# A hybrid S5 / gated DeltaNet / MoE layer: Toeplitz loads and input loads on another DMA queue, w_mod tiles in other buffers, S5's readout weights moved, one clearing on VectorE

## The chip, the cores and the metric

One core of one Trainium2 chip. The metric is device time in microseconds. The kernel before takes 1488.81 us (median of three runs).

## The reference, cut to what matters

One layer over 256 latent tokens and 256 context tokens, width 1024, float32. The computation, shortened:

```python
mod = silu(c) @ w_mod + b_mod          # shift, scale, gate of both norms; the same for c_ctx
h  = rmsnorm(x, norm1) * (1 + sc1) + sh1          # latent tokens
hc = rmsnorm(ctx, norm1) * (1 + csc1) + csh1      # context tokens
u, qkv, gate, b_raw, a_raw, br = split(h @ w_in)
q, k, v = split(silu(short_conv(qkv)))
ya = glu(s5(u))                        # bidirectional complex diagonal SSM, starts from the context's state
yb = gated_norm(gdn(q, k, v), gate)    # bidirectional chunked DeltaNet, a triangular solve per chunk of 64
x = x + gt1 * ((sig(br_a) * (ya @ w_branch_a) + sig(br_b) * (yb @ w_branch_b)) @ w_out)
x = x + gt2 * moe(rmsnorm(x, norm2) * (1 + sc2) + sh2)   # 32 experts, top 4
return rmsnorm(x, norm_f)
```

## The kernel before, in words

Weights stream from HBM in tiles of 128 x 2048 (1 MB), issued by SP. They land in the five `ld` buffers or in one of the 1 MB registers that `r()` names (`R0`, `PB`, `XC`, ...). A register or buffer comes free when its last reader is done, and a load for it waits until then.

**Start.** `mod1` multiplies silu(c) by eight tiles of `w_mod` (`wm`, line 226), adds `b_mod` into `modrow` and transposes it. `load_x` and `load_h` load and normalise the tokens and transpose them (`xn`, 32 transposes). `modulate` then forms the input `h` and its high part `hh`. From there on PE multiplies `h` and `hh` by tiles of `w_in` (`win`, line 609). ScalarE rounds each piece to its high part and VectorE takes the rest (`wsp`). Each projection `u`, `k`, `v`, `q`, `gate`, `br` is a run of blocks of 512 columns of weights. A block on all tokens is 24 products, and after `lat_only` (latent tokens alone) 16. Sixteen steps of the second `w_mod` half lie between blocks (`mod` in ORDER).

**S5.** `s5_prep` makes powers of the diagonal. `s5_P` writes the drive weights of direction 0 into registers PA and PB, of direction 1 into R2 and V (`pt` are the pieces that PE transposes). `s5_in` multiplies them with U, which goes through DRAM (`us`). `s5_R0` and `s5_R1` form the readout weights R from CC and PD, with 24 operations of 128x512 each on POOL (ENG_R). `s5_scan` runs on VectorE, `s5_steps` (31 steps on `XL`, which the scan fills) on POOL. `s5_K` multiplies BB with R (256 products) into `KS`, which ScalarE stores to DRAM in two halves (`kd`, line 543). `s5_T` loads the Toeplitz tiles T back from there with sixteen DMAs of 128 KB, eight from SP's and eight from ScalarE's queue (line 577). `s5_out` multiplies T with U, and R with XL.

**DeltaNet.** `l2k` normalises k (`sq` on ScalarE, `rnk` on POOL, transposes on PE), `l2q` does it for q (`rnq`). `gdn_a` makes the chunk matrix A, stores it (`ad`) and loads it as M. It clears Y on POOL (lines 1092 and 1093), and 31 steps on VectorE solve for Y. `yd` stores Y, `gdn_b1` reads it back as Yb. Eight scan steps follow, then the branches and `merge`.

**Experts.** `merge` starts the stream of 403 MB of expert weights. Tile after tile goes into a ring of 19 buffers (`WREG`), each as soon as its buffer is free.

**What sets the order.** SP's DMAs are issued in program order. On the other engines a scheduler fixes one static order from priorities. ORDER is the sequence of the program and `name@p*n` calls a part n times with its priority lowered by p. An engine works through its order without overtaking.

Of the kernel before, what the change touches and what calls it, by code (L numbers as in the profile page):

```python
# [27 lines left out]
class Kern:  # L28
# [166 lines left out]
    ENG_P, ENG_R, ENG_E = "GVGGVVVV", "GGGGGGGG", "VVGV"  # L195
    ORDER = """proj_ba u*5 mod*2 gdn_e k mod k mod k mod k mod s5_C s5_in0 s5_in1 s5_R0 s5_scan l2k gdn_a
        v mod v mod v mod v mod lat_only s5_steps s5_R1 q mod q mod q mod q mod l2q s5_K s5_T mod*2 gate*4
        br@3000*8 s5_out gdn_b0 br@3000*8 gdn_b1 s5_glu@500 ba@500*8"""

    def mod1(self):  # L200
# [9 lines left out]
        def run(cb, nb, tag):  # L210
# [3 lines left out]
            def step(j, b):  # L214
# [10 lines left out]
                t = self.ld("wm")  # L225
# [72 lines left out]
    def load_h(self):  # L298
# [3 lines left out]
        junk = self.r("H0", "junk")[:, :D]  # L302
# [56 lines left out]
    def s5_load(self):  # L359
        nc, I, wk = self.nc, self.I, self.wk  # L360

        self.L = self.r("R2", "L")[:, :768].rearrange("p (a b) -> p a b", b=32)
        nc.sync.dma_start(self.L[:, 0], dram(I["s5_lam_re"], 0, [[32, 128], [1, 32]]))
        nc.sync.dma_start(self.L[:, 1], dram(I["s5_lam_im"], 0, [[32, 128], [1, 32]]))
        for a in range(2):
            nc.sync.dma_start(self.L[64 * a:64 * a + 64, 2], dram(I["s5_log_step"], 32 * a, [[0, 64], [1, 32]]))
# [2 lines left out]
        for i, nm in enumerate(("s5_b_re", "s5_b_im")):
            nc.sync.dma_start(self.raw[:, i], dram(I[nm], 0, [[512, 128], [1, 512]]))  # L370

    def s5_loadc(self):
        for i, nm in enumerate(("s5_c_re", "s5_c_im")):
            self.nc.sync.dma_start(self.raw[:, 2 + i], dram(self.I[nm], 0, [[512, 128], [1, 512]]))
# [102 lines left out]
    def s5_R1(self):  # L477
        self.s5_R(1, ("R0", "R1"))
# [26 lines left out]
    def s5_K(self):  # L505
# [3 lines left out]
        KS = self.r("PB", "KS")  # L509
# [79 lines left out]
    S5L = 1  # L589
    WIN0 = 0  # L590
# [474 lines left out]
    def gdn_a(self):  # L1065
# [727 lines left out]
```

## Time and profile before

| | |
|---|---|
| runs of the kernel before, us | 1487.31, 1488.81, 1489.29 |
| profiled execution, its own time | 1497.49 us |
| its span | 1495.7 us |
| mean granted clock of PE | 0.948 |
| busy: PE, DVE, ACT, POOL | 1347.7, 572.4, 267.5, 210.7 us |
| DMA bytes | 474.06 MB |

The profiled execution took 8.68 us more than the median of the runs. Differences are read inside the profiled execution and then taken off the median. The timeline gives for a group of like instructions its start, its length and in brackets the idle time ahead of it with what ended it. The windows give busy time by engine in a stretch. The groups give busy time, mean length and idle time of all instructions of one kind.

### The profile page before, as it was taken

To read this page: it belongs to the slowest core of one execution; us is meant where nothing else is said; L and a number is where in the kernel's file an instruction comes from. 1 tells how busy PE (TensorE), PEld (TensorE's weight loads), DVE (VectorE), ACT (ScalarE), POOL (GpSimd) and SP (SyncE) were. 2 spreads that over 40 slices of the span, in tenths; PEclk is the share of its full clock that TensorE was granted. 3 is DMA by queue.
4 is the path that set the end of the run, shared out by engine and by line. 5 is a ranking of instruction groups with operands and counts; after the bars stand their busy time and mean duration, and the time that the engine had idled before them with its cause. 6 is when DMAs were issued, how large, how long until landed. Compare 5 with 4: busy or idle time off the path is not lost. (4 is left out here: it accounts for less than half of the span.)

```text
span 1495.7 us, 18843 instructions
## 1 busy us (share of the span) xinstructions
PE 1347.7 (90%) x7583; PEld 631.3 (42%) x7583; DVE 572.4 (38%) x1097; ACT 267.5 (18%) x592; POOL 210.7 (14%) x324
## 2 busy tenths in 40 slices
PE   4799796399989989999999999999999999999975
PEld 1365664277958543333333333333333333333221
DVE  4869988365334432223223123123222212221223
ACT  3443331124410011101111111111111101110001
POOL 1725687512000000000000000000000000000000
PEclk9799897699989989999999999999999999999996
DMA  9283162932184889999999999999999999999992
GB/s 336 75 215 131 68 197 59 191 100 78 61 204 179 305 317 381 422 421 420 419 421 421 420 420 420 421 420 420 420 421 421 420 420 421 421 421 420 420 420 109
DMA packets 92689, 474.06 MB, mean 317 GB/s; under 512 B 23984, under 2 KB 28317, under 8 KB 40757
## 3 DMA queue, kind: packets, MB, share of 16 engines
q1 hardware_dynamic: 72925, 461.11, 77.9%
q10 hardware_dynamic: 19672, 11.68, 3.7%
q8 instruction: 62, 1.02, 0.3%
q14 instruction: 30, 0.25, 0.0%
HBM read 468.61 MB, written 4.15 MB: 316 GB/s over the span
## 5 line engine op out<-in xcount | busy, mean ns | idle before, releaser
L79 PE MATMUL ps<-w,xT 128*64 128x512 f32 x2048 | 488.2, 602 | 6.5 <-DMA w<-in_w_gate_up_dram 6.4
L79 PEld LDWEIGHTS ps<-w,xT 128*64 128x64 f32 x2048 | 138.2, 137 | 269.8 <-issue 244.2
L79 PE MATMUL ps<-w,aT 128*64 128x512 f32 x1024 | 233.9, 600 | 10.5 <-DMA w<-in_w_down_dram 9.7
L1729 DVE SCALAR_TENSOR_TENSOR od<-ps,cs,gt 128x512 f32<-128x512 f32 x32 | 24.0, 751 | 478.0 <-PE ps L79 478.0
L79 PEld LDWEIGHTS ps<-w,aT 128*64 128x64 f32 x1024 | 72.1, 138 | 165.0 <-issue 128.2
L79 PE MATMUL ps<-h,wsp 128*128 128x512 f32 (+1 forms) x480 | 112.9, 375 | 2.9 <-DVE gx L94 2.0
L94 DVE TENSOR_TENSOR x<-x,ps 128x512 f32<-128x512 f32 x128 | 84.0, 684 | 65.8 <-PE ps L79 65.8
L1525 POOL CAST selsd<-biad 128x128 fp32r<-128x128 f32 x32 | 9.4, 294 | 700.0 <-PE ps L79 700.0
L97 ACT ACTIVATE odh<-od 128x512 fp32r<-128x512 f32 x31 | 19.5, 630 | 424.4 <-DVE od L1729 424.4
L79 PEld LDWEIGHTS ps<-h,wsp 128*128 128x128 f32 x480 | 82.0, 199 | 29.9 <-issue 12.4
L94 DVE TENSOR_TENSOR wsp<-win,wsp 128x512 fp32r<-128x512 f32 x72 | 58.5, 841 | 42.2 <-ACT wsp L97 41.9
L79 PE MATMUL ps<-h,oh 128*64 128x512 f32 x248 | 63.0, 604 | 0.0
L97 ACT ACTIVATE wsp<-win 128x512 fp32r<-128x512 f32 x72 | 41.3, 622 | 84.0 <-PE ps L79 42.4
L79 PE MATMUL ps<-hh,wsp 128*128 128x512 f32 x192 | 53.6, 411 | 1.3 <-DVE wsp L94 1.3
L97 ACT ACTIVATE sgm<-gt 128x512 f32<-128x512 f32 x32 | 20.1, 629 | 174.1 <-DVE gt L1702 174.1
L79 PE MATMUL ps<-wm,sc 128*32 128x512 f32 x192 | 34.4, 733 | 12.8 <-DMA wm<-in_w_mod_dram 12.8
L706 DVE SCALAR_TENSOR_TENSOR cacc<-raw,cols,cacc 128x512 f32<-128x512 f32 (+1 forms) x48 | 43.6, 908 | 3.2 <-ACT cacc L97 3.0
L1702 DVE TENSOR_SCALAR gt<-ps 128x512 f32<-128x512 f32 x32 | 22.1, 692 | 58.8 <-PE ps L79 58.8
L97 ACT ACTIVATE aT<-ps 128x512 f32<-128x512 f32 x32 | 19.1, 597 | 140.0 <-PE ps L83 140.0
L79 PEld LDWEIGHTS ps<-hh,wsp 128*128 128x128 f32 x192 | 35.1, 192 | 18.9 <-issue 10.0
L1525 POOL CAST selsg<-biad 128x256 fp32r<-128x256 f32 x32 | 13.9, 433 | 191.0 <-PE ps L79 184.8
L79 PE MATMUL ps<-odh,ST 64*128 64x512 f32 x124 | 31.7, 505 | 6.0 <-ACT odh L97 6.0
(370 smaller groups left out, 1497.2 us busy)
## 6 DMA issues: line engine op xcount, KB each, us to landing
w<-in_w_gate_up_dram SPq DMA_DIRECT2D x242, 1024.0 KB
w<-in_w_down_dram SPq DMA_DIRECT2D x121, 1024.0 KB
wm<-in_w_mod_dram SPq DMA_DIRECT2D x24, 1024.0 KB
win<-in_w_in_dram SPq DMA_DIRECT2D x18, 1024.0 KB
w<-in_w_gate_up_dram SPq DMA_DIRECT2D x28, 512.0 KB
w<-in_w_down_dram SPq DMA_DIRECT2D x14, 512.0 KB
wo<-in_w_out_dram SPq DMA_DIRECT2D x4, 1024.0 KB
wa<-in_w_branch_a_dram SPq DMA_DIRECT2D x4, 512.0 KB
```

The lines of the kernel that those rows point to most:

```text
L79: self.nc.tensor.matmul(out, lhsT, rhs, start=start, stop=stop, **kw)
L94: (eng or self.nc.vector).tensor_tensor(out, a, b, op=op)
L97: self.nc.scalar.activation(out, in_, func, **kw)
L706: nc.vector.scalar_tensor_tensor(acc[:, rows], rt[:, rows, k:k + 64], sc, acc[:, rows], op0=OP.mult, op1=OP.add)
L1525: nc.gpsimd.tensor_copy(v.rearrange("p (n s) -> p n s", s=CAP), dup[:, x:x + n, None].to_broadcast([128, n, CAP]))
L1702: V.tensor_scalar(gt, pz[0], 7.0, None, op0=OP.min)
L1729: V.scalar_tensor_tensor(od, self.pd, self.cs, k.gt2, op0=OP.mult, op1=OP.mult)
```

## The change

- `mod1`'s first five `w_mod` tiles go to the registers R0, R1, H0, H1 and GA, the last three to `ld`. Tokens, S5's small inputs and the second set of small vectors are loaded from ScalarE's queue. S5's c weights are loaded with its b weights. The loads of `wba` and of two `w_in` tiles stand right behind `w_mod`. `mod1`'s ending is a function of its own, called after `load_h`.
- `s5_P(1)` comes ahead of `s5_P(0)`, and `s5_C` and `s5_R0` come right behind both. Some of their operations change between POOL and VectorE (ENG_P), and one product on the DeltaNet side goes from POOL to VectorE (ENG_E).
- ORDER: `s5_R1` and `s5_steps` come ahead of v. `s5_K` and `s5_T` come ahead of q, where they stood behind `l2q`. `s5_out` and `gdn_b0` come ahead of the gates, whose priority is lowered like `br`'s.
- R1 goes to PB and R2, KS to R0, T to R0 and R1. The second XB goes to register K.
- All sixteen loads of T come from ScalarE's queue. Y is cleared on VectorE.

```diff
-        self.load_h()
+        self.s5_load()
+        self.smalls1()
         self.mod1()
         self.wins, self.winq, self.pair = self.win_order(), [], {}
+        self.ba_load()
         for _ in range(self.WIN0):
             self.win_load()
-        self.s5_loadc()
+        self.load_h()
+        self.mod1_end()
         self.modulate()
         self.s5_prep()
-        self.P = [self.s5_P(0), self.s5_P(1)]
+        self.P = [None, self.s5_P(1)]
+        self.P[0] = self.s5_P(0)
+        self.s5_C()
+        self.s5_R0()
...
-    ENG_P, ENG_R, ENG_E = "GVGGVVVV", "GGGGGGGG", "VVGV"
-    ORDER = """proj_ba u*5 mod*2 gdn_e k mod k mod k mod k mod s5_C s5_in0 s5_in1 s5_R0 s5_scan l2k gdn_a
-        v mod v mod v mod v mod lat_only s5_steps s5_R1 q mod q mod q mod q mod l2q s5_K s5_T mod*2 gate*4
-        br@3000*8 s5_out gdn_b0 br@3000*8 gdn_b1 s5_glu@500 ba@500*8"""
+    ENG_P, ENG_R, ENG_E = "GVGVVGVV", "GGGGGGGG", "VVVV"
+    ORDER = """proj_ba u*5 mod*2 gdn_e k mod k mod k mod k mod s5_in0 s5_in1 s5_scan l2k gdn_a s5_R1 s5_steps
+        v mod v mod v mod v mod lat_only s5_K s5_T q mod q mod q mod q mod l2q mod*2 s5_out gdn_b0
+        gate@1000*4 br@3000*16 gdn_b1 s5_glu@500 ba@500*8"""
...
-                t = self.ld("wm")
+                t = self.r(regs[j], "wm") if j < len(regs) else self.ld("wm")
...
-        for j, f in enumerate(run(0, 1, "p5")):
+        for f in run(0, 1, "p5", ("R0", "R1", "H0", "H1", "GA")):
             f()
-            if j == self.S5L:
-                self.s5_load()
-                self.smalls1()
...
-        self.rows(nc.sync, lambda t, a, b: self.xt[a:b, t], I["x"], True)
+        self.rows(nc.scalar, lambda t, a, b: self.xt[a:b, t], I["x"], True)
...
-        self.s5_R(1, ("R0", "R1"))
+        self.s5_R(1, ("PB", "R2"))
...
-        KS = self.r("PB", "KS")
+        KS = self.r("R0", "KS")
...
-        self.T = [self.r(x, "T").rearrange("p (g k) -> p g k", g=16) for x in ("PB", "R2")]
-        for hf, eng in ((0, nc.sync), (1, nc.scalar)):
+        self.T = [self.r(x, "T").rearrange("p (g k) -> p g k", g=16) for x in ("R0", "R1")]
+        for hf, eng in ((0, nc.scalar), (1, nc.scalar)):
...
-    WIN0 = 0
+    WIN0 = 2
...
-        nc.gpsimd.memset(Y, 0.0)
-        nc.gpsimd.memset(Y.rearrange("p i j -> p (i j)")[:, ::33], 1.0)
+        V.memset(Y, 0.0)
+        V.memset(Y.rearrange("p i j -> p (i j)")[:, ::33], 1.0)
...
-            X = self.r(("GA", "R3")[grp], "XB").rearrange("p (x i) -> p x i", i=128)
+            X = self.r(("GA", "K")[grp], "XB").rearrange("p (x i) -> p x i", i=128)
```

How it moves instructions, in three places. The first is PE's order at the start, before: the last `w_mod` group stands between two groups of transposes of S5's pieces (`pt`).

```order
L79 MATMUL ps<-wm,sc 32x512 x16
L83 MATMUL ps<-ident,pt_411 128x128 x4
L79 MATMUL ps<-wm,sc 32x512 x4
L83 MATMUL ps<-ident,pt_412 128x128 x4
L83 MATMUL ps<-ident,modrow 128x128 x4
L79 MATMUL ps<-hh_122,wba 32x512
```

The same place in the changed kernel:

```order
L79 MATMUL ps<-wm,sc 32x512 x8
L83 MATMUL ps<-ident,rows 128x128
L83 MATMUL ps<-ident,xn 128x128 x4
L83 MATMUL ps<-ident,pt_417 128x128 x4
L83 MATMUL ps<-ident,xn 128x128 x4
L83 MATMUL ps<-ident,modrow 128x128 x4
L83 MATMUL ps<-ident,xn 128x128 x8
L83 MATMUL ps<-ident,pt_418 128x128 x4
```

The last `w_mod` groups now stand ahead of S5's pieces, and one group of pieces, of the direction that is now made first, stands ahead of `modrow`.

The second place is PE's order ahead of T's products with U, before. BB with R is `s5_K`, `sq`, `rnq` belong to `l2q`, and vT are transposes for `gdn_b0`.

```order
L79 MATMUL ps<-ident,rnq 128x128 x8
L83 MATMUL ps<-ident,vT 128x128 x3
L79 MATMUL ps<-ident,vT 64x128 x4
L83 MATMUL ps<-ident,vT 128x128 x2
L79 MATMUL ps<-ident,vT 64x128 x2
L79 MATMUL ps<-T,U 32x128 x18
```

In the changed kernel `s5_K` (with `rnk` and the key products put among its rows) comes right behind v. Its first transposes of `rnk` stand behind 8 of its 256 products. From the second `q` block's end on the order is (h with `wsp` is q):

```order
L79 MATMUL ps<-wm,sc 32x512 x4
L79 MATMUL ps<-h_266,wsp 128x512 x4
L79 MATMUL ps<-h_266,wsp 128x256 x4
L79 MATMUL ps<-h_267,wsp 128x512 x4
L79 MATMUL ps<-h_267,wsp 128x256 x4
L79 MATMUL ps<-wm,sc 32x512 x4
L79 MATMUL ps<-h_266,wsp 128x512 x4
L79 MATMUL ps<-h_266,wsp 128x256 x4
L79 MATMUL ps<-wm,sc 32x512 x4
L79 MATMUL ps<-h_267,wsp 128x512 x4
L79 MATMUL ps<-h_266,wsp 128x512 x4
L79 MATMUL ps<-T,U 32x128 x4
```

The q blocks and three of the steps of `wm` now stand between `s5_K` and T, and `sq`, `rnq` and vT stand behind T.

The third place is ScalarE's order at T's loads, before. `KS`, `kd` belong to `s5_K`.

```order
L543 DMA kd<-KS 4x32x960
L97 ACTIVATE sq<-Q 128x256 x3
L97 ACTIVATE KS<-ps 128x4x112
L543 DMA kd<-KS 4x32x960
L577 DMA T<-kd 16x16x128 x8
L97 ACTIVATE wsp<-win 128x512 x2
L1101 DMA yd<-Y 128x1024
```

And in the changed kernel, where `ad` and M are DeltaNet's matrix, and `raw`, `cacc`, `cth` the short convolution of q:

```order
L1092 DMA ad<-A 32x32x32 x2
L1092 DMA ad<-At 32x32x32
L97 ACTIVATE KS<-ps 128x4x128
L1092 DMA ad<-At 32x32x32
L97 ACTIVATE KS<-ps 128x4x112
L546 DMA kd<-KS 4x32x960
L1094 DMA M<-ad 128x1024
L97 ACTIVATE raw_623<-ps 128x4x64
L97 ACTIVATE wsp<-win 128x512
L97 ACTIVATE cacc<-raw_623,cols 128x256
L580 DMA T<-kd 16x16x128 x16
L97 ACTIVATE cth<-cacc 128x256
```

All sixteen loads of T and the round trip of A now stand on ScalarE's queue, ahead of q's `cth` and of the next `wsp`.

## Rows read from the trace of the kernel before

**Rows 1.** Busy us by engine in three stretches, then PE clock, DMA share, GB/s.
```profile
20.00:40.00 20.00, 10.83 (x73) 4.89 (x69) 15.55 (x64) 5.64 (x11) 4.88 (x4) 0.80 1.02 420
260.00:280.00 20.00, 0.00 (x0) 0.00 (x0) 6.21 (x15) 1.15 (x2) 17.85 (x55) 0.52 0.99 93
600.00:1400.00 800.00, 779.68 (x3573) 274.23 (x3575) 202.74 (x360) 92.51 (x195) 19.76 (x56) 1.00 1.01 421
```

**Rows 2.** Timeline of PE in the experts: start, length, instructions, idle time and releaser.
```profile
1205.12 1.94 PE L79 MATMUL ps<-w,aT 128*64 128x512 f32 x8 [0.25 <-DMA w<-in_w_down_dram]
```

**Rows 3.** Timeline of SP's queue: the first expert weights, and the next eleven.
```profile
423.12 0.33 SPq L1439 DMA_DIRECT2D w<-in_w_gate_up_dram  x1
...
473.57 30.89 SPq L1439 DMA_DIRECT2D w<-in_w_gate_up_dram  x11
```

**Rows 4.** Timeline of PE at the start.
```profile
40.15 1.12 PE L83 MATMUL ps<-ident,pt 128*128 128x128 f32 x4 [5.78 <-POOL pt L94]
41.20 1.94 PE L79 MATMUL ps<-wm,sc 128*32 128x512 f32 x8
...
48.94 1.12 PE L83 MATMUL ps<-ident,modrow 128*128 128x128 f32 x4 [4.75 <-DVE modrow L94]
52.55 1.92 PE L79 MATMUL ps<-hh,wba 128*32 128x512 f32 x2 [2.50 <-ACT hh L97]
```

**Rows 5.** Timeline of PE from v's last two blocks to T's first product.
```profile
184.73 2.12 PE L79 MATMUL ps<-hh,wsp 128*128 128x512 f32 x8
...
196.65 2.13 PE L79 MATMUL ps<-kT 128*64 128x64 f32 x64
...
202.66 1.66 PE L79 MATMUL ps<-h,wsp 128*128 128x512 f32 x8
...
243.35 1.93 PE L79 MATMUL ps<-R,BB 64*32 64x128 f32 x32 [9.91 <-DVE KS L94]
...
249.38 1.48 PE L79 MATMUL ps<-R,BB 64*16 64x128 f32 x24
...
285.04 3.10 PE L79 MATMUL ps<-T,U 128*32 128x128 f32 x36 [26.67 <-DMA T<-kd]
```

**Rows 6.** Groups of PE's instructions between 200 and 260 us.
```profile
L79 PE MATMUL ps<-h,wsp 128*128 128x512 f32 (+1 forms) x68 | 16.9, 387 | 0.0
L79 PE MATMUL ps<-R,BB 64*16 64x128 f32 (+1 forms) x256 | 12.9, 312 | 12.6 <-DVE KS L94 9.9 <-POOL R L94 2.7
L79 PE MATMUL ps<-wm,sc 128*32 128x512 f32 x40 | 6.2, 696 | 0.0
L79 PE MATMUL ps<-ident,rnq 128*128 128x128 f32 x16 | 4.1, 441 | 0.9 <-POOL rnq L94 0.7 <-DVE Q L732 0.3
L79 PE MATMUL ps<-ones,sq 128*128 128x1 f32 x16 | 3.7, 355 | 0.0
```

**Rows 7.** Timeline of ScalarE and its DMA queue around T.
```profile
252.73 0.55 ACTq L543 DMA_DIRECT2D kd<-KS  x1
263.37 13.45 ACTq L577 DMA_DIRECT2D T<-kd  x8
276.87 1.15 ACT L97 ACTIVATE wsp<-win 128x512 fp32r<-128x512 f32 x2 [25.40 <-DMA T<-kd]
```

**Rows 8.** Groups of POOL's instructions between 100 and 260 us.
```profile
L94 POOL TENSOR_TENSOR R<-R,rtmp 128x512 f32<-128x512 f32 x16 | 25.8, 1627 | 0.0
L94 POOL TENSOR_TENSOR rtmp<-CC,PD 128x512 f32<-128x512 f32 x16 | 21.4, 1354 | 13.5 <-PE ps L79 13.4
L94 POOL TENSOR_TENSOR R<-CC,PD 128x512 f32<-128x512 f32 x16 | 19.3, 1239 | 29.3 <-ACT CC L97 29.3
```

**Rows 9.** Timeline of DVE: one operation alone and beside POOL.
```profile
136.16 0.68 DVE L94 TENSOR_TENSOR A<-A,gsm 128x512 f32<-128x512 f32 x1
...
142.87 1.78 DVE L94 TENSOR_TENSOR A<-A,gsm 128x512 f32<-128x512 f32 x1
```

**Rows 10.** Timeline of POOL: Y's clearing.
```profile
222.70 0.95 POOL L1092 MEMSET Y<- 128x1024 f32 x1
```

More of the change, by code (lines that the diff above doesn't have):

```diff
@@ L128, in consts, with smalls @@
         nc.gpsimd.memset(self.mhalf, -0.5)
-    def smalls(self, src):
+    def smalls(self, src, eng):
         nc, I = self.nc, self.I
@@ L137, in smalls @@
         for n, k in src:
-            nc.sync.dma_start(rows[r:r + k], dram(I[n], 0, [[128, k], [1, 128]]))
+            eng.dma_start(rows[r:r + k], dram(I[n], 0, [[128, k], [1, 128]]))
             self.col[n] = r0 + r
@@ L149, in smalls0 @@
         self.cols = self.con.tile([128, 128], F32, name="cols")
-        self.smalls(self.VECS[:2])
+        self.smalls(self.VECS[:2], self.nc.sync)
     def smalls1(self):
-        self.smalls(self.VECS[2:])
+        self.smalls(self.VECS[2:], self.nc.scalar)
         r = self.col["gdn_norm"]
@@ L208, in mod1, with run @@
         w = I["w_mod"]
-        def run(cb, nb, tag):
+        def run(cb, nb, tag, regs=()):
             ps = []
@@ L241, in mod1, with mod1_end @@
         self.mod_run = run
-        for j, f in enumerate(run(0, 1, "p5")):
+        for f in run(0, 1, "p5", ("R0", "R1", "H0", "H1", "GA")):
             f()
-            if j == self.S5L:
-                self.s5_load()
-                self.smalls1()
+    def mod1_end(self):
+        nc = self.nc
         nc.gpsimd.memset(self.sc[:, :, 2], 0.0)
@@ L281, in load_x @@
         self.ct = self.r("K", "ct").rearrange("p (a d) -> p a d", a=2)
-        self.rows(nc.sync, lambda t, a, b: self.xt[a:b, t], I["x"], True)
+        self.rows(nc.scalar, lambda t, a, b: self.xt[a:b, t], I["x"], True)
         for a in range(2):
-            nc.sync.dma_start(self.ct[:, a], dram(I["ctx"], 128 * D * a, [[D, 128], [1, D]]))
+            nc.scalar.dma_start(self.ct[:, a], dram(I["ctx"], 128 * D * a, [[D, 128], [1, D]]))
     def seat(self, c):
@@ L301, in load_h @@
         ss = self.w([128, 4], "ss")
-        junk = self.r("H0", "junk")[:, :D]
+        junk = self.r("XL", "junk")[:, :D]
         src = [ct[:, 0], ct[:, 1], self.xt[:, 0], self.xt[:, 1]]
@@ L324, in modulate @@
         def modulate():
+            h = [self.r("H0", "h0"), self.r("H1", "h1")]
+            hi = [self.r("R0", "hh0"), self.r("R1", "hh1")]
+            self.hx = h, hi
+            self.hl = [part(h, j).bitcast(F32R) for j in range(8)]
+            self.hh = [part(hi, j).bitcast(F32R) for j in range(8)]
             for j in range(8):
@@ L334, in load_h @@
         self.modulate = modulate
-        self.hx = h, hi
-        self.hl = [part(h, j).bitcast(F32R) for j in range(8)]
-        self.hh = [part(hi, j).bitcast(F32R) for j in range(8)]
     def lat_only(self):
@@ L362, in s5_load @@
         self.L = self.r("R2", "L")[:, :768].rearrange("p (a b) -> p a b", b=32)
-        nc.sync.dma_start(self.L[:, 0], dram(I["s5_lam_re"], 0, [[32, 128], [1, 32]]))
-        nc.sync.dma_start(self.L[:, 1], dram(I["s5_lam_im"], 0, [[32, 128], [1, 32]]))
+        nc.scalar.dma_start(self.L[:, 0], dram(I["s5_lam_re"], 0, [[32, 128], [1, 32]]))
+        nc.scalar.dma_start(self.L[:, 1], dram(I["s5_lam_im"], 0, [[32, 128], [1, 32]]))
         for a in range(2):
-            nc.sync.dma_start(self.L[64 * a:64 * a + 64, 2], dram(I["s5_log_step"], 32 * a, [[0, 64], [1, 32]]))
+            nc.scalar.dma_start(self.L[64 * a:64 * a + 64, 2], dram(I["s5_log_step"], 32 * a, [[0, 64], [1, 32]]))
         self.raw = self.r("Q", "s5raw").rearrange("p (i x c) -> p i x c", i=4, c=16)
[L369 to L374, printed above, removed]
+        for i, nm in enumerate(("s5_b_re", "s5_b_im", "s5_c_re", "s5_c_im")):
+            nc.scalar.dma_start(self.raw[:, i], dram(I[nm], 0, [[512, 128], [1, 512]]))
     def cmul(self, outr, outi, ar, ai, br, bi, tmp, eng=None):
@@ L667, in proj_u, with ba_load @@
         return (lambda b=b: step(b) for b in range(5))
+    def ba_load(self):
+        w = self.wba = self.w([128, 8, 32], "wba", "c2")
+        self.nc.sync.dma_start(w.rearrange("p j c -> p (j c)"), dram(self.I["w_in"], 18 * 128 * 2048, [[256, 128], [1, 256]]))
     def proj_ba(self):
-        w = self.w([128, 8, 32], "wba", "c2")
-        self.nc.sync.dma_start(w.rearrange("p j c -> p (j c)"), dram(self.I["w_in"], 18 * 128 * 2048, [[256, 128], [1, 256]]))
+        w = self.wba
         p = self.pt("p")
```

3 lines of the change are left out of this document (removed).

## The prediction

> **What bounds the kernel now.** I read the windows first. From 600 us to 1400 us the DMA engines are full, at a share of 1.01 and 421 GB/s [rows 1]. The weights of the experts pass in that stretch, and PE, though busy for 779.68 of 800 us, ends up waiting for each tile, as at 1205.12 us, where it waits for a `w_down` tile [rows 2]. So the end of the kernel is the start of this stream plus its length. SP's timeline shows what holds the start back: the first expert tile goes out at 423.12 us, the next eleven only from 473.57 us [rows 3], when the DeltaNet scan and the merge give their registers back. A microsecond gained ahead of the scan should therefore come off the end whole. Every part of the change but XB's register lies ahead of the scan.
>
> The front is bound by PE, so I look for PE's idle time. There are two large holes. At the start, PE begins the projections at 52.55 us [rows 4]. The last `w_mod` group had run only at 41.20 us, behind transposes that waited 5.78 us for POOL, and after it come 4.75 us for `modrow`. The second hole is T: PE waits 26.67 us up to 285.04 us [rows 5], after a wait of 9.91 us inside `s5_K`. From 260 to 280 us PE does nothing at all, and DMA is busy for 0.99 of that time while it moves only 93 GB/s [rows 1]. T's sixteen loads are slow by themselves, not late in a queue.
>
> **The change part by part.**
>
> *The start.* Ahead of the projections must come eight `w_mod` tiles (8.4 MB), the tokens (2.1 MB) and S5's b and c (1.0 MB). At the 420 GB/s of the second 20 us [rows 1] these 11.5 MB take 27.5 us. With about 2 us until the first issue and 2 us for the last group (1.94 us in [rows 4]) that group ends at about 31.5 us, and 33.5 us if the first tiles come no faster than PE and the queue let them. Before, it ended at 41.20 + 1.94 = 43.1 us. I take 33.5 and keep the rest of the way, 43.1 to 52.55 us, as it was. The projections start at 42.9 us, **9.6 us earlier**. Bounds: 4 us, if the S5 pieces that still stand ahead of `modrow` come as late as now (40.15 us) and only `modrow`'s wait goes, and 14.4 us, if `modrow`'s 4.75 us go as well.
>
> *Up to the end of v.* The same blocks, in much the same order. I carry the waits over unchanged. The first q product comes at 202.66 us before [rows 5], and after it will be 202.66 - 9.6 = 193 us when v ends and `s5_K` can start. The key products (two groups of 2.13 us as in [rows 5]) and the transposes of `rnk` (4.1 us, like `rnq`'s in [rows 6]) move from v into `s5_K`. I leave v's end as it is, though they no longer stand ahead of it: that is worth up to 8.4 us and belongs to the upper bound.
>
> *POOL and `s5_K`.* The 48 operations of R0 and R1 are busy for 25.8 + 21.4 + 19.3 = 66.5 us [rows 8], 1.39 us each. R0 no longer waits for CC until 108 us. R1 writes PB and R2, which the drive products still read. In the changed order these end in the first and second v block. Counted back from 193 us over three blocks (a block with its step is (202.66 - 184.73 - 2 x 2.13)/2 = 6.8 us, [rows 5]) and some 14 us of small products (`sq` 3.7 us [rows 6], groups of 64 at 2.13 us), PB is free at about 158 us. R1's first eight operations end at 169 us, fifteen more at 190 us. Then come D (four operations) and `rnk`, at the same price 6.9 us, so `rnk` is there at 197 us. PE asks for it eight products into `s5_K`, at 193.5 us: a **wait of 3 us** (rounded down, since D's pieces are smaller). `s5_K` itself has 12.9 us [rows 6], 4.1 us of transposes and 4.3 us of key products. It ends at 193 + 3 + 21.3 = 217.3 us. Before, it ended at 249.38 + 1.48 = 250.9 us.
>
> *T.* From there to the first product with T it took 285.04 - 250.9 = 34.1 us: the store of `kd` (252.73 us), 10.6 us until the first load could go, then the loads [rows 7]. I keep that: T's first product at 251.4 us. Queue: before, eight loads took 13.45 us to issue from ScalarE [rows 7] while SP issued the other eight. If issuing were the limit, sixteen from one queue would take 13.45 us more. If the DMA engines are, nothing is added, and the 0.99 share at 93 GB/s [rows 1] is nearest to that. I take 0 and keep 13.45 for the range. The Trainium skill ("Trainium Kernel Development and Optimization", Key Constraints) says that DMAs of all queues run on the same 16 engines, and that issuing from several only saves issue time. By that rule T gains nothing and loses nothing either, and the trace agrees with its 0.99.
>
> *What fills the wait.* Now two and a half q blocks and three steps stand between `s5_K` and T. A q block is 16 of the 68 products that take 16.9 us, 4.0 us, and a step 6.2/5 = 1.24 us [rows 6]: 13.7 us of the 34.1 are work. But ScalarE's next `wsp` and `cth` stand behind the sixteen loads. Before, the first `wsp` came at 276.87 us [rows 7], 8.2 us ahead of T's product, so the second half of the q work just fits into that end. PE waits some 20 us for T instead of 26.67. Behind T now comes what stood ahead of it: the rest of q (4 x 4.0 + 4 x 1.24 - 13.7 = 7.3 us), `sq` (3.7 us) and `rnq` (4.1 us), 15.1 us. The same state is reached at 251.4 + 15.1 = 266.5 us, which was 285.04. **Gain 18.5 us**, the start's 9.6 among it.
>
> *The rest.* Clearing Y costs 0.95 us on POOL [rows 10] and at most 1.78 us on VectorE, the longest 128x512 operation in [rows 9]. It lies ahead of the solve, and Y is read by PE only after many gate and `br` blocks, so I price it at nothing. If that cover went, it would cost 1 us. The gates and `br` behind `gdn_b0` are the same work and fill the waits there. XB in K is read before the scan, as GA and R3 are, and nothing loads K before that: nothing. The solve is cut by q's convolution, which waits for `cth`. Late next is `rnq`, behind that solve. The 9 us of filler behind T (rest of q, `mod`) and R's products with XL should cover it, and 0 to 8 us stay for the range. I take 1 us for it.
>
> **Sum.** 1497.49 - 18.5 + 1 = 1480.0 us in the profiled execution's own time. That execution stood 8.68 us over the median, so the forecast is **1471.3 us**. With the bounds (start 4 to 14.4, a wait of 0 to 14 for `rnk`, T 0 to 13.45, behind T 0 to 8, not all at once) this case alone spans 1462 to 1483.
>
> **The rivals.**
>
> *POOL decides, and the kernel is slower: 1498 us.* R1 now goes ahead of `rnk`, on an engine that does not overtake, and PE stands still at the first transposes. One operation of VectorE took 0.68 us alone and 1.78 us beside POOL [rows 9], so POOL's may stretch as well. If R1 starts only when both registers are free (174 us) and its 23 operations take 1.78 us each, they end at 215 us, D and `rnk` at 224 us. Then PE waits 30 us instead of 3, and 18.5 us of gain become a loss of 8.5: 1488.81 + 9.5 with the 1 us above. It decides from `rnk` later than 214 us on. Against it: the mean of 1.39 us already holds such stretched operations. The Trainium skill ("SBUF — State Buffer", Who interferes with whom) says that a VectorE instruction with two SBUF inputs and a POOL instruction that reads SBUF block each other, and this trace agrees with 0.68 against 1.78 us.
>
> *More stalls go: 1450 us.* If R1 is done before v ends, `rnk` is no wait, the key products' 8.4 us come off v's end, and q fills all of T's wait but 8 us (20 - 8 = 12 us). 18.5 + 3 + 8.4 + 12 = 41.9, less the 3 that such a chain gives back at `rnq`: 39 us, 1450. Against it: ScalarE's queue is blocked by T as before [rows 7].
>
> *Only the start is gained: 1480 us.* If q cannot run behind the blocked `wsp`, what `s5_K`'s earlier place brings is lost at T again, and the start's 9.6 us less the 1 us at `rnq` are left.
>
> *The change doesn't reach the end: 1489 us.* If something else released the experts' registers, the front would not matter. Against it: the eleven tiles that wait until 473.57 us [rows 3].
>
> **How the numbers follow.** Main case 0.46, more stalls gone 0.25, only the start 0.14, POOL decides 0.10, no effect 0.05. Two runs of this kernel can tell about 0.2% (3 us) apart from no change. Faster by more: 0.46 + 0.25 + 0.14 = 0.85. Within: 0.05. Slower: 0.10. The range goes from 1448 us, below the second rival, to 1486 us, above the third, and leaves out the two last cases and a little below. The main case's own range is 1462 to 1483.
>
> **What would show it.** Right: the first `wba` product near 43 us, T's first product near 251 us with a wait of about 20 us, POOL's `rnk` near 197 us, SP's eleven expert tiles near 456 us. Wrong: a wait of PE for `rnk` of over 10 us, T's loads taking over 30 us, or a new wait for `rnq` or Y between T and the scan. If the first expert tiles come early and the end doesn't, the first paragraph is wrong.

## The result: one per cent slower, and the profile after

The changed kernel takes 1502.11 us (median of four runs, 1501.79 to 1502.45). The kernel before took 1488.06 us beside it. The ratio is 1.0098, with an interval of 1.008 to 1.0115. The forecast was 1471.3 us with a range of 1448 to 1486: the sign is wrong. The profiled execution after took 1502.27 us (span 1500.5), so it stands at its median. The one of before stood 8.7 us over its own.

The windows of the changed kernel, over two of the stretches of [rows 1]:

```profile
20.00:40.00 20.00, 5.17 (x28) 1.46 (x32) 0.74 (x3) 6.76 (x12) 0.53 (x2) 1.00 0.94 372
600.00:1400.00 800.00, 778.98 (x3567) 274.30 (x3565) 201.48 (x358) 92.60 (x195) 19.85 (x55) 1.00 1.01 420
```

The experts' stretch is the same to 1 GB/s. From 20 to 40 us PE does half of what it did (5.17 us for 10.83) and VectorE next to nothing (0.74 us for 15.55). SP's queue, against [rows 3]:

```profile
441.15 0.40 SPq L1444 DMA_DIRECT2D w<-in_w_gate_up_dram  x1
...
471.33 37.82 SPq L1444 DMA_DIRECT2D w<-in_w_gate_up_dram  x11
523.32 5.48 SPq L1444 DMA_DIRECT2D w<-in_w_down_dram  x4
```

From the four `w_down` tiles to the end it takes 1500.5 - 523.32 = 977.2 us. Before, it was 977.1 (518.63 us of 1495.7). The loss lies ahead of them. PE's timeline at the start, against [rows 4]:

```profile
34.83 7.12 PE L79 MATMUL ps<-wm,sc 128*32 128x512 f32 x40 [27.38 <-DMA modrow<-in_b_mod_dram]
...
61.79 1.12 PE L83 MATMUL ps<-ident,pt 128*128 128x128 f32 x4 [13.26 <-DVE pt L94]
...
71.91 1.92 PE L79 MATMUL ps<-hh,wba 128*32 128x512 f32 x2 [1.79 <-ACT hh L97]
```

The projections were to begin 9.6 us earlier and begin 19.4 us later. PE does not touch `w_mod` before 34.83 us, and then runs five tiles at once: they had long been there (in e5, with the same loads, it uses the first at 11.67 us). Up to 61.79 us it then waits 13.26 us for VectorE's S5 pieces. ScalarE's timeline tells why (ACTq rows are the DMAs it issues, from the same instruction stream):

```profile
0.80 1.65 ACTq L303 DMA_DIRECT2D xt<-in_x_dram  x3
2.49 1.08 ACTq L291 DMA_DIRECT2D ct<-in_ctx_dram  x2
6.55 0.34 ACTq L370 DMA_DIRECT2D L<-in_s_lam_re_dram  x1
...
12.82 4.23 ACTq L373 DMA_DIRECT2D L<-in_s_log_step_dram  x2
...
32.81 0.23 ACTq L138 DMA_DIRECT2D rows<-in_gdn_norm_dram  x1
...
34.41 0.32 ACT L97 ACTIVATE sc<-cols 128x8 f32<-128x8 f32 x2
34.63 1.04 ACT L97 ACTIVATE junk<-ct 128x1024 f32<-128x1024 f32 x1
```

The tokens' five loads go out at once. The eleven small ones behind them need until 33 us, and ScalarE's first activation, silu(c), runs at 34.41 us, behind all sixteen. The program's own waits explain it. The layer that builds the program deals the DMAs of both queues out to eight semaphores, and a load waits until the one that had its semaphore before has landed:

```
L370 DMA L<-in_s_lam_re_dram 128x32 [waits DMAHW1_49]
L371 DMA L<-in_s_lam_im_dram 128x32 [waits DMAHW3_49]
L373 DMA L<-in_s_log_step_dram 64x32 [waits DMAHW5_49]
L373 DMA L<-in_s_log_step_dram 64x32 [waits DMAHW7_49]
L377 DMA s5raw<-in_s_b_re_dram 128x512 [waits DMAHW1_49]
```

Beside eight 1 MB tiles even the 16 KB of `L` land late: the next load on its semaphore, `s5raw`, goes out at 19.20 us, 12.65 us after it, and VectorE's first operation on this part of `L` starts at the same time:

```profile
19.20 0.18 DVE L399 TENSOR_SCALAR L<-L 128x32 f32<-128x32 f32 x1 [11.54 <-DMA L<-in_s_lam_re_dram]
```

A waiting DMA holds everything behind it in ScalarE's stream. The squares of the tokens, exp and sine of S5, and with them VectorE and POOL, stand behind it. The tokens' data were there long before: the two loads of line 373 wait on the semaphores that the two loads of `ct` had used (5 and 7), and both had gone out by 17.05 us. The squares of `ct` run at 34.63 us.

The middle part, in PE's timeline, against [rows 5]:

```profile
223.72 0.66 PE L79 MATMUL ps<-R,BB 64*32 64x128 f32 x16
...
236.11 2.08 PE L79 MATMUL ps<-ident,rnk 128*128 128x128 f32 x8 [7.91 <-DVE kT L94]
...
266.10 2.90 PE L79 MATMUL ps<-h,wsp 128*128 128x512 f32 x8 [6.37 <-DVE raw L94]
...
281.37 1.94 PE L79 MATMUL ps<-wm,sc 128*32 128x512 f32 x8 [12.37 <-DMA wm<-in_w_mod_dram]
287.59 3.78 PE L79 MATMUL ps<-h,wsp 128*128 128x512 f32 x8 [4.29 <-ACT wsp L97]
291.30 1.07 PE L79 MATMUL ps<-T,U 128*32 128x128 f32 x8
```

T's first product comes at 291.30 us, 6.3 us later than before: of the 19.4 us, two thirds are made up by then. Between `s5_K` and T PE waits 6.37 + 12.37 + 4.29 = 23.0 us. The longest of these waits comes from ScalarE's queue too. In the program SP's next load of `wm` waits on a semaphore that DeltaNet's load of M, on ScalarE's queue, had used before it. SP's wait for it, in total, how often, and the longest, in us:

```profile
SPq L232 <- DMA M<-ad: 18.2, 1, 18.2
```

SP issues the tile at 273.36 us, and PE starts on it at 281.37 us. ScalarE at T, against [rows 7]:

```profile
256.78 0.60 ACT L97 ACTIVATE KS<-ps 128x512 f32<-128x512 f32 x1 [10.56 <-DMA ad<-A]
...
258.99 3.63 ACTq L546 DMA_DIRECT2D kd<-KS  x1
...
272.11 14.18 ACTq L580 DMA_DIRECT2D T<-kd  x16
286.33 0.42 ACT L97 ACTIVATE cth<-cacc 128x256 f32<-128x256 f32 x1 [19.84 <-DMA T<-kd]
```

And POOL, against [rows 8]:

```profile
175.38 5.74 POOL L94 TENSOR_TENSOR R<-CC,PD 128x512 f32<-128x512 f32 x4 [22.01 <-PE ps L79]
...
219.57 2.97 POOL L94 TENSOR_TENSOR rnk<-rnk,mhalf 128x16 f32<-128x16 f32 x1 [7.10 <-DVE rnk L729]
```

VectorE does its part of `rnk` at 219.25 us. The last product with `sq` that it needs had ended at 203.03 us on PE, and from then on VectorE was busy without a gap, with S5's scan and DeltaNet's A among other things (16.20 of 16.20 us; busy us of PE, PE's weight loads, VectorE, ScalarE and POOL):

```profile
203.00:219.20 16.20, 8.74 (x33) 5.83 (x33) 16.20 (x27) 0.28 (x1) 9.41 (x8) 0.74 0.11 28
```

### The profile page after: what moved, and what is told of

Its sections match the earlier page's. It is cut to its first block, busy times and chain, and to the rows that moved or that the text cites. A ratio compares the mean times of both kernels' runs of the same rounds, so it can differ in the third digit from the quotient of the medians.

```text
span 1500.5 us, 18842 instructions
## 1 busy us (share of the span) xinstructions
PE 1338.3 (89%) x7583; PEld 628.5 (42%) x7583; DVE 567.1 (38%) x1102; ACT 267.7 (18%) x592; POOL 199.7 (13%) x319
## 5 line engine op out<-in xcount | busy, mean ns | idle before, releaser
L79 PE MATMUL ps<-hh,wsp 128*128 128x512 f32 x192 | 59.6, 451 | 17.6 <-ACT raw L97 9.9
L79 PE MATMUL ps<-wm,sc 128*32 128x512 f32 x192 | 30.1, 702 | 46.8 <-DMA modrow<-in_b_mod_dram 27.4
L79 PEld LDWEIGHTS ps<-hh,wsp 128*128 128x128 f32 x192 | 40.1, 217 | 37.1 <-ACT raw L97 11.2
L711 DVE SCALAR_TENSOR_TENSOR cacc<-raw,cols,cacc 128x512 f32<-128x512 f32 (+1 forms) x48 | 37.2, 776 | 1.1 <-ACT cacc L97 0.6
```

The source lines that it names most:

```text
L79: self.nc.tensor.matmul(out, lhsT, rhs, start=start, stop=stop, **kw)
L711: nc.vector.scalar_tensor_tensor(acc[:, rows], rt[:, rows, k:k + 64], sc, acc[:, rows], op0=OP.mult, op1=OP.add)
```

## The experiments

The theory after the result: **A**, ScalarE's queue is held by the loads at the start, and the whole start is late with it, while the middle part gains. Rivals: **B**, the loads compete for the same bytes per second whatever queue they are on, and **C**, the middle part itself loses (T on one queue, or R1 ahead of `rnk`). All kernels were timed beside the kernel before. The expectations speak of fourteen loads; they are sixteen.

The table gives, from each kernel's own profile in us: the first product with `wba`, the first with T, the issue of the four `w_down` tiles, what lies between the first and the third, and the span. Ratios are those of the timed runs.

| kernel | projections | T | `w_down` | between | span | ratio to before, interval |
|---|---|---|---|---|---|---|
| before | 52.55 | 285.04 | 518.63 | 466.1 | 1495.7 | |
| before, second profile (e15) | 51.88 | 283.85 | 512.00 | 460.1 | 1488.8 | |
| changed | 71.91 | 291.30 | 523.32 | 451.4 | 1500.5 | 1.0098, 1.008 to 1.0115 |
| e1 inputs on SP | 51.53 | 280.48 | 502.03 | 450.5 | 1480.1 | 0.9948, 0.9918 to 0.9978 |
| e2 start alone | 72.62 | 308.15 | 539.56 | 466.9 | 1513.7 | 1.0138, 1.0066 to 1.021 |
| e3 middle alone | 48.75 | 278.09 | 505.65 | 456.9 | 1484.4 | 0.997, 0.9939 to 1.0001 |
| e4 T in halves | 71.59 | 291.85 | 535.15 | 463.6 | 1509.7 | 1.0144, 1.0076 to 1.0211 |
| e5 silu first | 73.14 | 298.20 | 525.03 | 451.9 | 1501.2 | 1.0069, 1.0045 to 1.0093 |
| e6 tokens alone on ScalarE | 53.94 | 271.63 | 492.85 | 438.9 | 1469.5 | 0.9884, 0.9847 to 0.9922 |
| e8 T late on SP | 51.62 | 261.90 | 497.80 | 446.2 | 1477.1 | 0.9886, 0.9851 to 0.9921 |
| e9 one product back to POOL | 51.24 | 282.00 | 505.18 | 453.9 | 1481.7 | 0.992, 0.989 to 0.9949 |
| e10 small loads on ScalarE | 59.66 | 290.49 | 512.01 | 452.4 | 1490.2 | 0.9999, 0.9973 to 1.0024 |
| e11 start alone, mended | 45.22 | 273.30 | 501.61 | 456.4 | 1480.3 | 1.0001, 0.9981 to 1.002 |
| e12 middle alone, T late | 49.05 | 263.32 | 505.26 | 456.2 | 1480.2 | 0.9963, 0.9939 to 0.9986 |
| e13 both mends | 54.98 | 257.98 | 490.31 | 435.3 | 1468.0 | 0.9899, 0.9868 to 0.993 |
| e14 both, old order of S5's pieces | 45.60 | 260.92 | 491.65 | 446.1 | 1471.0 | 0.9896, 0.9844 to 0.9948 |

Two profiles of the kernel before differ by 6 us in the fourth column, so smaller differences there tell nothing by themselves. The timed runs of that kernel lie between 1481.24 and 1499.05 us.

**e1: all inputs back on SP, ahead of `w_mod`.** (The same edit in all seven places.)

```diff
-        self.rows(nc.scalar, lambda t, a, b: self.xt[a:b, t], I["x"], True)
+        self.rows(nc.sync, lambda t, a, b: self.xt[a:b, t], I["x"], True)
```

> The changed kernel with the tokens, S5's small inputs and the second set of small vectors issued by SP again, ahead of the eight w_mod tiles. Theory A (ScalarE's queue): in the changed kernel fourteen loads stand on ScalarE ahead of its first activation and are held up one by one by the w_mod tiles, so the silu that w_mod's products need runs at 34.4 us instead of 6.1 us. Then here the silu is back at 6 to 9 us, the projections start at 45 to 52 us instead of 71.9 us, and the time is 1475 to 1485 us, below both kernels. Theory B (bandwidth): the eight w_mod tiles that go out at once take the DMA engines from the small inputs, whoever issues them; then the projections still start after 65 us and the time stays above 1495 us.

1482.59 us. The projections begin at 51.53 us, 20.4 us earlier than in the changed kernel, the span is 20.4 us shorter, and what lies between is the same (450.5 and 451.4). So where the inputs are issued is worth 20 us, and that alone makes the change slower. The bytes are the same, but e1 also puts the inputs ahead of the tiles instead of beside them. So e1 alone does not tell A from B. That late data alone are not the cause is shown by `ct`, which had landed by 17.05 us in the changed kernel and was read at 34.63, and again by e5.

**e2 and e3: each half of the change alone.** e2 takes the middle part back, as below and with ORDER, R1, KS, T, Y and XB as before. e3 is the kernel before with just these edits the other way round.

```diff
-    ENG_P, ENG_R, ENG_E = "GVGVVGVV", "GGGGGGGG", "VVVV"
+    ENG_P, ENG_R, ENG_E = "GVGGVVVV", "GGGGGGGG", "VVGV"
...
-        self.P = [None, self.s5_P(1)]
-        self.P[0] = self.s5_P(0)
-        self.s5_C()
-        self.s5_R0()
+        self.P = [self.s5_P(0), self.s5_P(1)]
```

> Only the first part of the change: ScalarE's queue for the inputs, w_mod in registers, early w_in tiles, load_h behind mod1. Order, readout weights, KS, T, Y and XB are as before. Theory A: the whole loss lies here, the projections start near 72 us and the time is 1502 to 1510 us. Theory C (the loss lies in the middle part: order, T on one queue, R1): 1475 to 1492 us.

> Only the second part of the change: order, s5_P's order, R1, KS and T in other registers, T's loads on ScalarE, Y on VectorE, XB; the start is as before. Theory A: faster than before by 5 to 15 us, 1473 to 1483 us. Theory C: slower than before, 1495 to 1510 us.

1513.28 and 1484.59 us. The start alone loses 1.4 per cent, and lies 3 us above the range expected. The middle part does not lose: its interval ends at no change, so a gain of some 4 us is likely but not certain, and less than expected. That leaves of C nothing that could make the kernel slower. Its trace has the waits that the prediction feared, with another cause. PE's, ScalarE's and POOL's timelines of e3:

```profile
193.21 3.78 PE L79 MATMUL ps<-ident,rnk 128*128 128x128 f32 x16 [12.68 <-POOL rnk L94]
```

```profile
252.08 22.30 ACTq L580 DMA_DIRECT2D T<-kd  x16
274.43 0.42 ACT L97 ACTIVATE cth<-cacc 128x256 f32<-128x256 f32 x1 [29.91 <-DMA T<-kd]
```

```profile
189.86 3.30 POOL L94 TENSOR_TENSOR rnk<-rnk,mhalf 128x16 f32<-128x16 f32 x1 [9.57 <-DVE rnk L727]
```

PE waits 12.68 us for `rnk`, but POOL was done with R1 and itself waited 9.57 us for VectorE.

**e4: T in halves again, in the changed kernel.**

```diff
-        for hf, eng in ((0, nc.scalar), (1, nc.scalar)):
+        for hf, eng in ((0, nc.sync), (1, nc.scalar)):
```

> The changed kernel with eight of T's loads on SP's queue again. Theory A: within 4 us of the changed kernel (1498 to 1506 us), because T's sixteen loads are bound by the DMA engines. Theory C, as far as T is concerned: sixteen loads on one queue cost 8 to 13 us, 1489 to 1494 us.

1511.17 us, 21.5 over the kernel before beside it (the changed kernel: 14.1), where at most 4 us more were expected. The intervals of the two overlap, so the runs alone don't settle it. In the profile, with the same start, the way to `w_down` is 12.2 us longer. SP's queue, and PE behind it:

```profile
217.76 1.84 SPq L518 DMA_DIRECT2D dsk<-in_s_d_dram  x4
270.28 12.47 SPq L580 DMA_DIRECT2D T<-kd  x8
283.40 0.35 SPq L611 DMA_DIRECT2D win<-in_w_in_dram  x1
```

```profile
291.85 1.07 PE L79 MATMUL ps<-T,U 128*32 128x128 f32 x8 [41.42 <-DMA T<-kd]
```

From 219.6 us on SP waits for `kd`, with q's weights behind T in its order. So q cannot fill PE's wait, which is 41.42 us. In the new order T has to be off SP, or behind q.

**e5: silu ahead of the loads.** silu(c) is written right behind `smalls0`; the scheduler puts it behind six loads.

```diff
         self.smalls(self.VECS[:2], self.nc.sync)
+        self.sc = self.con.tile([128, 8, 34], F32, name="sc")
...
+        self.act(self.sc[:, :, 1], self.cols[:, c0:c0 + 8], AF.Silu)
```

> The changed kernel, but silu(c) is written ahead of the loads on ScalarE, so that the scheduler places it behind six loads of that queue instead of fourteen. Theory A (whatever stands behind the loads on ScalarE's queue is held, and it is the squares of the tokens and S5's exp and sine that PE waits for, not silu): silu at 7 to 10 us and the first w_mod product by 15 us, but the squares still behind 30 us, the projections (first product with wba) at 66 to 72 us, time 1493 to 1503. Rival A2 (PE's 27 us of waiting for silu is the whole loss, the rest of the start only follows from it): projections at or ahead of 55 us, time 1478 to 1486.

1501.42 us. PE's and ScalarE's timelines:

```profile
11.67 1.93 PE L79 MATMUL ps<-wm,sc 128*32 128x512 f32 x8 [4.28 <-DMA wm<-in_w_mod_dram]
...
73.14 1.92 PE L79 MATMUL ps<-hh,wba 128*32 128x512 f32 x4 [4.62 <-ACT hraw L97]
```

```profile
8.98 0.31 ACT L97 ACTIVATE sc<-cols 128x8 f32<-128x8 f32 x2
...
32.99 1.16 ACTq L228 DMA_DIRECT2D modrow<-in_b_mod_dram  x2
34.20 1.06 ACT L97 ACTIVATE junk<-ct 128x1024 f32<-128x1024 f32 x1 [24.91 <-DMA modrow<-in_b_mod_dram]
```

PE's wait of 27 us is gone, so it was for silu(c); the load of `modrow`, which its row names, goes out at 32.99 us here too. But the projections gain nothing: they begin at 73.14 us. (The ratio is 0.3 per cent under the changed kernel's, and the intervals overlap.) The squares of `ct` need nothing but `ct`, whose loads went out at 2.45 us and had landed by 17 us, as in the changed kernel, and still run at 34.20. It is the blocked stream, not late data.

**e6 and e10: which of the loads.** e6 leaves the tokens' five loads on ScalarE and puts the eleven small ones on SP, in five places like these two; e10 does the opposite.

```diff
-        self.smalls(self.VECS[2:], self.nc.scalar)
+        self.smalls(self.VECS[2:], self.nc.sync)
...
-            nc.scalar.dma_start(self.raw[:, i], dram(I[nm], 0, [[512, 128], [1, 512]]))
+            nc.sync.dma_start(self.raw[:, i], dram(I[nm], 0, [[512, 128], [1, 512]]))
```

> The changed kernel, but only the five loads of the tokens stay on ScalarE's queue; S5's inputs and the second small vectors go out from SP ahead of w_mod. Theory A (a few loads pass at once, since eight may be under way; it is those beyond that are held one by one behind the 1 MB tiles): silu by 8 us, squares by 15 us, projections at 46 to 53 us, time 1478 to 1486. Rival A3 (any load on ScalarE's queue beside w_mod holds that engine): silu behind 15 us, time 1490 or more.

> The changed kernel with the tokens' five loads back on SP ahead of w_mod; S5's inputs and the second small vectors, eleven loads of some 2 KB to 256 KB, stay on ScalarE's queue. Theory A (it is how many loads stand on ScalarE's queue ahead of its first activation, each held by the loads under way on SP): the eleven are issued over more than 12 us, silu at 12 to 28 us, the projections at 56 to 68 us, time 1486 to 1498, between e6 and the changed kernel. Rival (it is the tokens on ScalarE's queue that cost, since they are big): silu by 9 us, projections at 50 to 54 us, time 1472 to 1483.

1472.75 and 1489.67 us. ScalarE's timeline, first of e6, then of e10:

```profile
8.39 0.22 ACT L97 ACTIVATE sc<-cols 128x8 f32<-128x8 f32 x1
...
8.61 1.04 ACT L97 ACTIVATE junk<-ct 128x1024 f32<-128x1024 f32 x1
```

```profile
4.29 0.33 ACTq L377 DMA_DIRECT2D s5raw<-in_s_c_re_dram  x1
7.01 0.33 ACTq L377 DMA_DIRECT2D s5raw<-in_s_c_im_dram  x1
...
15.92 0.32 ACT L97 ACTIVATE sc<-cols 128x8 f32<-128x8 f32 x2
```

In e6 the squares run at 8.61 us. In e10 seven loads pass by 4.6 us and the rest at 7.01 to 14.31, with silu at 15.92 and the projections at 59.66. So 2.1 MB of tokens in five loads cost ScalarE little and 1.1 MB in eleven loads hold silu back by 7.5 us: their number counts, not their size. In e10's program the last four of the eleven wait on semaphores of earlier loads among the eleven, not of the tokens'. e6 beats both kernels, and by more than expected.

**e8, e12 and e13: T's loads on SP, behind q.** e8 is e1 with this edit, e12 is e3 with it, e13 is e6 with it.

```diff
-        v mod v mod v mod v mod lat_only s5_K s5_T q mod q mod q mod q mod l2q mod*2 s5_out gdn_b0
+        v mod v mod v mod v mod lat_only s5_K q mod q mod q mod q mod l2q s5_T mod*2 s5_out gdn_b0
...
-        for hf, eng in ((0, nc.scalar), (1, nc.scalar)):
+        for hf, eng in ((0, nc.sync), (1, nc.sync)):
```

> The changed kernel with its inputs on SP ahead of w_mod (as in e1) and with T's sixteen loads on SP, written behind the q blocks and l2q instead of ahead of them, so that neither q's weights nor ScalarE's wsp and cth stand behind them. If what e1 still lost between 245 and 280 us (PE waits of 4.1, 2.2 and 15.0 us) comes from ScalarE's queue being held by T's loads: those waits are under 5 us in sum, T's first product with U at 262 to 274 us, time 1466 to 1478, 5 to 15 us under e1. Rival: the loads of T are what is slow, and the wait only moves from wsp to T itself: PE waits over 12 us for T, time 1478 to 1486. Rival on the other side: the gates' weights, now behind T on SP, come late: 1486 or more.

> The middle part of the change alone, on the start of the kernel before (as in e3), with T's sixteen loads on SP behind the q blocks and l2q (as in e8). If T's loads on ScalarE's queue held the middle part back by what e8 gained over e1, it is 5 to 14 us under e3's 1484.6: 1470 to 1480, ratio 0.985 to 0.993, PE's waits for wsp and raw between 230 and 290 us under 10 us in sum. Rival: the waits only move to T: 1481 to 1488.

> The changed kernel with both mends: S5's inputs and small vectors on SP (as in e6), T's loads on SP behind q (as in e8). If the two losses lie one behind the other they add: 1464 to 1471, ratio 0.980 to 0.986. Rival: e6 already met most of what e8 met, by another order of the same rows: 1471 to 1477, as e6 or e8 alone.

1475.05, 1482.88 and 1471.57 us. T's first product comes at 258 to 263 us, 14 to 19 us earlier than without the edit. Of that, the way to `w_down` shows 4.3 us in e8, 3.6 in e13 and 0.7 in e12, no more than scatter. e8's ratio is 0.6 per cent under e1's, with intervals that just overlap; e12's is e3's, and e13's is e6's, so the two mends don't add. PE's row in e8:

```profile
261.90 1.07 PE L79 MATMUL ps<-T,U 128*32 128x128 f32 x8 [9.42 <-DMA T<-kd]
```

Where q stands ahead of T, PE still waits 9.42 us for T. So ScalarE's held queue at T is a small part of the matter. e8's time is as expected, but not its waits: 4.29 us for `wm` and the 9.42 for T are left, where under 5 in sum were expected. In e12 and e13 the rivals' times came true.

**e9: one DeltaNet product back on POOL, in e1.**

```diff
-    ENG_P, ENG_R, ENG_E = "GVGVVGVV", "GGGGGGGG", "VVVV"
+    ENG_P, ENG_R, ENG_E = "GVGVVGVV", "GGGGGGGG", "VVGV"
```

> The changed kernel with its inputs on SP (as in e1) and the one product on the DeltaNet side back from VectorE to POOL. If VectorE is what makes rnk late (in the kernel with the middle part alone POOL's rnk waited 9.6 us for VectorE), rnk comes 3 to 8 us earlier and the time is 2 to 6 us under e1. If POOL's R1 gates rnk, as the prediction had it, the product delays R1 and rnk further: time 0 to 4 us over e1.

1480.02 us. Its interval overlaps e1's: inconclusive. POOL's `rnk` comes at 179.62 us, 1.6 us earlier than in e1, where 3 to 8 were expected. What VectorE's load costs at `rnk` was not isolated.

**e11 and e14: what the start is worth with free queues.** e11 is e2 with e6's queues. e14 is e13 with the old order of the drive weights:

```diff
-        self.P = [None, self.s5_P(1)]
-        self.P[0] = self.s5_P(0)
+        self.P = [self.s5_P(0), self.s5_P(1)]
```

> The start of the changed kernel alone (middle part as before), with S5's inputs and the second small vectors back on SP as in e6. If the start's repair is worth what e6 gained on the changed kernel and the two parts add, it is 22 to 32 us under e2's 1513: 1481 to 1491, a ratio to before of 0.990 to 1.0, and the start is by itself a small gain or none, since the projections still begin within 2 us of where they did before. Rival: the start is good for its forecast 9.6 us: ratio under 0.990, wba ahead of 45 us.

> The kernel of e13 with the drive weights of direction 0 written ahead of direction 1 again, as before the change. In e11, which has that order, the projections began at 45.2 us, in e13 at some 55 us, because eleven groups of S5's pieces stand ahead of them. If those groups are what the start still loses: projections at 44 to 47 us, and if nothing behind takes it back 1460 to 1467, ratio 0.976 to 0.984. Rival: S5's drive of direction 1 and R1 then come later and rnk or s5_K waits for them, so that the earlier start is given back by v's end: 1468 to 1476, as e13.

1488.59 and 1473.51 us. In both the projections begin at 45 us, so the new order of S5's pieces (nine groups, not eleven, stand ahead of the projections in e13) costs 9 us there. But e14 is no faster than e13: its first product with T comes 2.9 us later, although its projections begin 9.4 us earlier. POOL's and PE's rows of e14:

```profile
193.58 3.36 POOL L94 TENSOR_TENSOR rnk<-rnk,mhalf 128x16 f32<-128x16 f32 x1 [11.47 <-DVE rnk L728]
```

```profile
106.07 3.50 PE L79 MATMUL ps<-hh,wsp 128*128 128x512 f32 x8 [8.13 <-ACT raw L97]
...
196.99 3.78 PE L79 MATMUL ps<-ident,rnk 128*128 128x128 f32 x16 [11.64 <-POOL rnk L94]
```

The earlier start is given back in several waits, not in one. PE waits 8.13 and then 3.16 us for ScalarE's `raw`, 11.64 us for `rnk`, which POOL gets from VectorE, and 4.47 us for VectorE's `kT`. e13 has no wait of over 1 us for `raw`, and one of 9.73 us for `kT` ahead of its transposes of `rnk`. From the projections to T PE is idle for 52.0 of 215.3 us in e14 and for 41.0 of 203.0 us in e13. Ahead of e14's `rnk`, too, VectorE is the engine that is full: it is busy for 20.80 of the 22.00 us from PE's last product with `sq` (to 171.4 us) to its own part of `rnk`. e11's ratio is 1.0001: by the runs the start alone is worth nothing, although its profile begins the projections 7 us earlier. That profile is of the fastest of its ten runs (1481.98 us), so its `w_down` at 501.61 us is early for it.

**e15: the kernel before, profiled again.**

> The kernel before, profiled again, since the profiled execution behind the prediction stood 8.7 us over the median. If that surplus lay in the front, ahead of the experts, the span is 1485 to 1491, the stretch from the four w_down tiles on SP's queue to the end is 977 us within 2 as in all other traces, and PE's wait for T is 18 to 27 us. If it lay in the experts' stream, that stretch is under 972 us and the front is as in the first profile within 2 us.

1490.54 us. PE's row at T and SP's two:

```profile
283.85 3.10 PE L79 MATMUL ps<-T,U 128*32 128x128 f32 x36 [25.95 <-DMA T<-kd]
```

```profile
466.86 30.96 SPq L1439 DMA_DIRECT2D w<-in_w_gate_up_dram  x11
512.00 5.48 SPq L1439 DMA_DIRECT2D w<-in_w_down_dram  x4
```

Up to T the two profiles differ by 1.2 us, up to the expert tiles by 6.7 us, and from `w_down` to the end by 0.3 us. (In all sixteen traces this last stretch takes 974 to 979 us.) T's wait of 26 us is the usual one. What scatters lies between T and the experts.

## Why the prediction was wrong

- **The start** is the step that failed: the last `w_mod` group at 33.5 us and the projections at 42.9 us, 9.6 us earlier. I counted bytes per second and the order on SP and PE, and let ScalarE's sixteen loads cost nothing on ScalarE, without a reason. They held it for 33 us: plus 19.4 us instead of minus 9.6. e1 takes this back, e5 and e10 show how. The lower bound of 4 us did not cover it, since no rival held a loss at the start. Even with free queues the 9.6 us are not there: the projections begin at 51 to 55 us with the change's order of S5's pieces (e1, e6, e13), and at 45 us with the old one (e11, e14). In the changed kernel three groups of pieces stand ahead of them (61.79 and 68.15 us); with ScalarE free the scheduler puts seven to nine there.
- **Up to the end of v** held in sum, and by luck: from the projections to `s5_K` 150.1 us were carried over, and 223.72 - 71.91 = 151.8 were measured. The waits were not the ones carried over. The key products' and transposes' 8.4 us did leave v, and new waits took their place: 6.83 and 3.06 us for `raw`, 7.46 us for VectorE's `wsp`.
- **POOL and `s5_K`.** The wait was put at 3 us, for `rnk` behind R1 on POOL. In the changed kernel POOL is done in time with all of R1 that stands ahead, and waits itself, 7.10 us for VectorE, which is busy without a gap. No term held VectorE's load. PE's wait is 7.91 us, for VectorE's `kT`. From the projections to `s5_K`'s end 179.8 us (251.70 - 71.91) were needed, 5.4 more than forecast (217.3 - 42.9). The rival in which POOL decides came near the time, 1498, for a reason that the traces deny.
- **T.** 34.1 us were carried over, 291.30 - 251.70 = 39.6 were measured. The second piece of KS waited 10.56 us on ScalarE behind the stores of `ad`, so the last `kd` went out at 258.99 us. The one queue itself costs little: sixteen loads took 14.18 us to issue, eight took 13.45 us before. That the term is near 0 and not 13.45 was right here; in e3 the sixteen took 22.30 us. But that SP has to be rid of T for q to run I did not see, and it is worth 7 us by e4's runs, 12 by its profile; e4's interval overlaps the changed kernel's, so the size is not certain.
- **What fills the wait, and the rest.** PE's waits ahead of T add up to 23.0 us, where some 20 were forecast. But the longest, 12.37 us, is for a `wm` tile that SP could not issue because of M, a path that the prediction did not have. In sum the middle part was sized about right. It was to gain 18.5 - 9.6 - 1 = 7.9 us between the projections and the experts. The way to `w_down` went from 466.1 to 451.4 us against the first profile of before, and by 8.7 us against the second, whose 1490.54 us are near the median of 1489.5 beside it. Minus 20.0 at the start (71.91 for 51.88) and plus 8.7 behind it make 11.3 of the 11.7 us between the spans (1500.5 and 1488.8). That the sum fits is luck, since two errors cancel. Between the projections and T 24.0 us were to be gained (232.5 to 208.5), and it was 13.1 (219.4). Behind T 15.1 + 1 us were to be given back, and T to `w_down` took 232.0 us, where the two profiles of before have 233.6 and 228.2. Why the work moved behind T cost so little is open.
- **The sum's base.** All differences were read inside an execution 8.7 us over the median. e15 says that its surplus lay behind T, where no term was read. It did no harm. But two runs do not tell 3 us apart, as the prediction has it: the runs of the kernel before span 18 us.
- The rule of the Trainium skill ("Trainium Kernel Development and Optimization", Key Constraints), that issuing from several engines only saves issue time, was cited for T. The changed kernel's 14.18 against 13.45 us agree with it, e3's 22.30 us less so. The 33 us that the loads cost ScalarE at the start are not issue time: they are waits for semaphores, and the prediction had no term for them.

Open: why an earlier start alone gives nothing (e11), and why e6's way to `w_down` is 11.6 us shorter than e1's, with a start 2.4 us later. The two differ only in the tokens' queue and in the static order that follows from it. That VectorE is full ahead of `rnk` is read from the traces; no run shows what taking work off it there would gain (e9).

## What to carry to other kernels

A DMA moved to another engine's queue is not free there: it can wait, and every instruction behind it waits with it. So look in the program at what the load waits for, and at what that engine must do first. Five large loads on ScalarE cost little here; with eleven small ones behind them, beside a stream of 1 MB tiles, it was 20 us. Where loads of two queues share semaphores, a load that stands on one can hold the other, as M held SP for 18.2 us. And a transfer that waits for data made in the kernel belongs behind the loads that are to fill the wait, or on a queue where nothing is due.

## What was not expected of the hardware

- Small loads are slow beside large ones: two loads of 16 KB at 6.55 and 9.06 us, and the loads that reuse their semaphores go out 12.65 and 12.69 us later (19.20, 21.75), beside the `w_mod` tiles. In e10, where the first of them goes out at 0.80 us, ahead of the tiles, VectorE uses it at 2.63 us.
- The sixteen loads of T took 14.18 us to issue in the changed kernel, 22.30 us in e3 and 11.31 us from SP in e8. The number of loads does not set it.
- Two executions of one kernel, 6.9 us apart in span, agree to 1.2 us up to T and to 0.3 us in the experts. The scatter has a place. 3.0 of the 5.5 us between T and the experts arise from 305 to 318 us: PE waits 1.99 us for VectorE's `gx` in the first and 0.60 us in the second, and the products of R with XL behind that take 8.70 and 7.43 us. The granted clock from 310 to 320 us is 0.90 in the first and 1.00 in the second.
